# A one-core transformer layer: half 0 of its first projection without GpSimd, x's second half loaded later, and the later adaLN pieces summed or read out one step later

## The chip, the cores and the metric

The kernel runs on one core of a Trainium2 chip. The metric is the time of one execution in microseconds (us). A core has TensorE (PE in the profile), VectorE (DVE), ScalarE (ACT), GpSimd (POOL) and SyncE (SP), which here only issues loads and stores. All work on SBUF and, for matmul results, on PSUM; each engine takes its own instructions strictly in order and waits for others by semaphores.

## What is computed

One layer with 1024 tokens of width 1024, all in float32. A conditioning vector c gives six modulation vectors; x is normalised, scaled and shifted, goes through one input projection (for forgetting attention: fq, fk, fv, og and 8 forget columns; for retention: rq, rk, rv, rg; 512 columns each), two kinds of attention, an output projection and a squared-ReLU MLP.

```python
c_act = jax.nn.silu(c)
mod = jnp.einsum('bd,de->be', c_act, w_ada[l]) + b_ada[l]
shift_m, scale_m, gate_m, shift_f, scale_f, gate_f = jnp.split(mod, N_MOD, axis=-1)
h = _rms(x) * (1.0 + scale_m) + shift_m
proj = jnp.einsum('bsd,de->bse', h, w_in[l])
...  # forgetting attention on fq fk fv, retention on rq rk rv, gated by og and rg
x = x + gate_m * jnp.einsum('bse,ed->bsd', mixed, w_out[l])
h = _rms(x) * (1.0 + scale_f) + shift_f
u = jnp.square(jax.nn.relu(jnp.einsum('bsd,df->bsf', h, w_mlp_in[l])))
x = x + gate_f * jnp.einsum('bsf,fd->bsd', u, w_mlp_out[l])
```

## The kernel before

**Matmuls.** A float32 product is made as three products of halves: each operand is split into a rounded part (hi) and a remainder (lo), and PE adds hi x hi, hi x lo and lo x hi into one PSUM bank (L291 to L293). `split_w` makes the two halves of a tile of w_in: ACT casts the hi half (L134), DVE or POOL subtracts it for the lo half (L135).

**The first block.** Eight pieces `wam` of w_ada (k = 0 to 7, shift and scale columns of one block of 128, 1 MB each as two loads, L174) are summed on DVE with the elements of c as factors (`ada_sum`: L208 twice, L211 six times, then L573), and PE sums over the partitions with a column of ones (`ada_cols`, L217 to `mps`); DVE adds the bias (L219). x comes in four pairs of 128-token tiles (`load_x`, L183, two loads of 512 KB each). `norm_x` squares a tile on ACT (L248), and DVE and POOL make its factor (L249, L131), which DVE applies (L251). `make_hT(k, half)` transposes four tiles on PE (L263 to `tp`); ACT scales and shifts them into `h` (L265), DVE casts the hi half of `hT` (L267), and POOL subtracts for the lo half (L268). Then `proj_group("rg", ...)` runs over the eight k: four token tiles by three products, 12 matmuls in a step; half 0 is the first 512 tokens, half 1 the others. In half 0 the lo half of w_in's tiles is POOL's work, everywhere else DVE's. `first_stage(k)` is the hook that, one step ahead, loads piece k+4, sums piece k and makes its hT; at k = 2 and 3 it loads x's second half.

**The stages after it.** `forget_logits` (L396 to L409, `fp`), then rq, rk, rv, fq, fk, og, fv by the same routine, each two halves of eight steps, retention's chunks between them. The other 32 adaLN columns come meanwhile as 22 pieces `wa`: `plan(at, n, d_sum, d_col)` puts the load of a piece on step `at`, its sum on DVE (L232, L234) `d_sum` steps later, its column on PE (L239) and bias (L241) `d_col` steps later. Ten pieces are double (256 columns, 1 MB, two buffers), at every fourth step; twelve are single (512 KB, one buffer), at every fifth. Their loads are issued on ACT's queue (L229).

**What sets the order.** A list scheduler orders each engine's instructions from the program's data flow; `tc.keep_in_program_order` ties an instruction to its place in the code. From about 475 us on (the attention sweep) the order is written out by hand. SP's loads are issued in order too, and each waits for the eighth load before it. Buffers that loads and splits wait for: tiles of w_in (`raw`, two, each with two steps), split tiles (`f4`, five, which the retention gain and the rotary table `cs` share).

Of the kernel before, what the change touches and what calls it, by code (L numbers as in the profile page):

```python
# [13 lines left out]
AF = mybir.ActivationFunctionType  # L14
ALU = mybir.AluOpType
# [9 lines left out]
FH, FD = 8, 64  # L25
# [24 lines left out]
def tile_block(  # L50
# [20 lines left out]
    V, A, G, T, Q = nc.vector, nc.scalar, nc.gpsimd, nc.tensor, nc.sync  # L71
# [21 lines left out]
    def f32(ap):  # L93
        return ap.bitcast(F32)
# [10 lines left out]
    def cols(n):  # L105
        used[0] += n
        return sm[:, used[0] - n : used[0]]

    ones, mhalf, e_base, qkg, kgc, bfc = (cols(1) for _ in range(6))
    r_x, c_sb, c_act = cols(8), cols(8), cols(8)  # L110
    rc = cols(12)
# [7 lines left out]
    def mod(m, k):  # L119
        return mcol[:, 8 * m + k : 8 * m + k + 1]  # L120
# [12 lines left out]
    def split_w(raw_ap, h_ap, l_ap, eng=V):  # L133
        A.copy(h_ap, raw_ap)  # L134
        eng.tensor_tensor(l_ap, raw_ap, f32(h_ap), op=ALU.subtract)  # L135
# [23 lines left out]
    def rbank(name):  # L159
        turn.append(turn.pop(0))  # L160
        return turn[-1](name)
# [9 lines left out]
    def load_ada_m(k):  # L171
        ada_m[k] = s8([P, 8, 2, P], f"wam{k}")
        for m in range(2):
            Q.dma_start(ada_m[k][:, :, m, :], wada_v[:, :, m * D + k * P : m * D + (k + 1) * P])  # L174
# [5 lines left out]
    def load_x(g):  # L180
        xg[g] = s8([P, 2, D], f"x{g}")
        for i in range(2):
            Q.dma_start(xg[g][:, i, :], x_v[g][:, i, :])  # L183
# [21 lines left out]
    def ada_sum(w):  # L205

        for j in range(2):
            V.tensor_scalar(w[:, j], w[:, j], c_act[:, j : j + 1], None, op0=ALU.mult)  # L208
        for j in range(2, 8):
            a = w[:, j % 2]  # L210
            V.scalar_tensor_tensor(a, w[:, j], c_act[:, j : j + 1], a, op0=ALU.mult, op1=ALU.add)  # L211
# [9 lines left out]
    def ada_stages(m, k, n):  # L221


        w = (mr if n > 1 else ra)([P, 8, n * P], f"wa{m}_{k}")

        def load():

            at = m * D + k * P
            tc.keep_in_program_order(A.dma_start(w, wada_v[:, :, at : at + n * P]))  # L229

        def sums():
            tc.keep_in_program_order(V.tensor_scalar(w[:, 0], w[:, 0], c_act[:, 0:1], None, op0=ALU.mult))  # L232
            for j in range(1, 8):
                V.scalar_tensor_tensor(w[:, 0], w[:, j], c_act[:, j : j + 1], w[:, 0], op0=ALU.mult, op1=ALU.add)  # L234

        def cols_():
            ps = xbank(f"mps{m}_{k}")
            for i in range(n):
                T.matmul(ps[:, i : i + 1], w[:, 0, i * P : (i + 1) * P], ones, start=True, stop=True)  # L239
            at = slice(8 * m + k, 8 * m + k + n)  # L240
            V.tensor_tensor(mcol[:, at], ps[:, 0:n], bT[:, at], op=ALU.add)  # L241

        return load, sums, cols_
# [11 lines left out]
    def make_hT(k, half):  # L255

        if k not in hT:
            hT[k] = s8([P, 2, S], f"hT{k}", F32R)
        ht = hT[k]
        tp = rbank(f"tp{k}_{half}")  # L260
        for i in range(4):
            t = 4 * half + i
            T.transpose(tp[:, i * P : (i + 1) * P], xg[t // 2][:, t % 2, k * P : (k + 1) * P], ident)  # L263
        h32 = t2([P, CH], f"h32_{k}_{half}")
        A.activation(h32, tp, AF.Identity, bias=mod(0, k), scale=mod(1, k))  # L265
        hs = slice(half * CH, (half + 1) * CH)
        V.tensor_copy(ht[:, 0, hs], h32)  # L267
        G.tensor_tensor(ht[:, 1, hs], h32, f32(ht[:, 0, hs]), op=ALU.subtract)  # L268

    def load_win(k, col, name):  # L270
        wr = raw([P, 2, CH], f"wr_{name}_{k}")
        Q.dma_start(wr, win_v[:, k : k + 2, col : col + CH])
        return wr

    def proj_group(name, col, half, evac, hook=None, banks=None):

        toks = range(4 * half, 4 * half + 4)
        ps, wr = {}, None
        for k in range(NK):
            if hook:  # L280
                hook(k)
            if k % 2 == 0:
                wr = early.pop(0) if early else load_win(k, col, f"{name}{half}")
            ws = f4([P, 2, CH], f"ws_{name}{half}_{k}", F32R)
            split_w(wr[:, k % 2, :], ws[:, 0, :], ws[:, 1, :], G if name == "rg" and half == 0 else V)
            for n, t in enumerate(toks):
                if k == 0:
                    ps[t] = (banks[n] if banks else bank)(f"pp_{name}_{t}")
                hh = hT[k][:, 0, t * P : (t + 1) * P]
                hl = hT[k][:, 1, t * P : (t + 1) * P]  # L290
                T.matmul(ps[t], hh, ws[:, 0, :], start=(k == 0), stop=False)  # L291
                T.matmul(ps[t], hh, ws[:, 1, :], start=False, stop=False)
                T.matmul(ps[t], hl, ws[:, 0, :], start=False, stop=(k == NK - 1))  # L293
        for t in toks:
            evac(t, ps[t])
# [5 lines left out]
    def copy_out(t, dst, src):  # L301
        if t % 2 == 0:
            A.copy(dst, src)
        else:
            V.tensor_copy(dst, src)
# [4 lines left out]
    def nat_tile(name, t):  # L310
        if (name, t // 4) not in nat:
            nat[name, t // 4] = s8([P, 4, CH], f"{name}{t // 4}")
        return nat[name, t // 4][:, t % 4, :]
# [33 lines left out]
    tabs = {}  # L347

    def evac_rope(name):
        def go(t, ps):  # L350
            d = nat_tile(name, t)
            if name == "rk":

                V.tensor_tensor(
                    d.rearrange("p (h d) -> p h d", d=RD),
                    ps.rearrange("p (h d) -> p h d", d=RD),
                    rc[:, 0:4].unsqueeze(2).to_broadcast([P, RH, RD]),
                    op=ALU.mult,
                )
            else:  # L360
                copy_out(t, d, ps)
            dv = d.rearrange("p (a d) -> p a d", d=64)
            ac = r2([P, 2 * RH, 64], f"ac_{name}{t}")
            as_ = r2([P, 2 * RH, 64], f"as_{name}{t}")
            cs = tabs["cs"]
            G.tensor_tensor(ac, dv, cs[:, t, 0:64].unsqueeze(1).to_broadcast([P, 2 * RH, 64]), op=ALU.mult)
            G.tensor_tensor(as_, dv, cs[:, t, 64:128].unsqueeze(1).to_broadcast([P, 2 * RH, 64]), op=ALU.mult)
            V.tensor_tensor(dv[:, 0::2, :], ac[:, 0::2, :], as_[:, 1::2, :], op=ALU.subtract)
            V.tensor_tensor(dv[:, 1::2, :], as_[:, 0::2, :], ac[:, 1::2, :], op=ALU.add)

        return go

    def load_gain(g):
        t = f4([P, CH], f"gain_{g.tensor.name}")
        Q.dma_start(t, g.partition_broadcast(P))
        return t
# [139 lines left out]
    ret = retention()  # L516
# [6 lines left out]
    def plan(at, n, d_sum, d_col):  # L523
        m, k = cols_left[0]
        del cols_left[:n]
        stages = []

        def begin():
            stages.extend(ada_stages(m, k, n))
            stages[0]()  # L530

        todo[at].append(begin)
        todo[at + d_sum].append(lambda: stages[1]())
        todo[at + d_col].insert(0, lambda: stages[2]())

    for n in range(10):
        plan(4 * n, 2, 4, 6)
    for n in range(12):
        plan(41 + 5 * n, 1, 3, 5)
    assert not cols_left  # L540
    todo = [[]] + todo

# [20 lines left out]
        return go  # L563

    def first_stage(k):
        if k == 2:
            load_x(2)
        if k == 3:
            load_x(3)
        if k + 4 < NK:  # L570
            load_ada_m(k + 4)
        ada_sum(ada_m[k])
        V.tensor_tensor(ada_m[k][:, 0], ada_m[k][:, 0], ada_m[k][:, 1], op=ALU.add)  # L573
        ada_cols(ada_m[k], [0, 1], k, 1)
        make_hT(k, 0)

    for t in range(4):
        norm_x(t)
    tabs["ret"] = load_gain(ret_gain)
    proj_group("rg", OFF_R + 3 * RW, 0, evac_rg, ahead(first_stage))  # L580
    for t in range(4, NT):
        norm_x(t)
    proj_group("rg", OFF_R + 3 * RW, 1, evac_rg, ahead(lambda k: make_hT(k, 1)))
    Q.dma_start(rc, rconst)
    for r in range(2):
        Q.dma_start(qkg[r * FD : (r + 1) * FD, :], q_gain.unsqueeze(1))
        Q.dma_start(kgc[r * FD : (r + 1) * FD, :], k_gain.unsqueeze(1))
    Q.dma_start(bfc[:FH, :], b_forget.unsqueeze(1))
    V.scalar_tensor_tensor(qkg, qkg, 1.0 / math.sqrt(FD), kgc, op0=ALU.mult, op1=ALU.mult)
    tabs["cs"] = f4([P, NT, P], "cs")  # L590
    Q.dma_start(tabs["cs"], rope.rearrange("(t p) e -> p t e", p=P))
# [464 lines left out]
    for e in range(NE):  # L1056
# [25 lines left out]
        for fs in steps:  # L1082
            ws = [load_up(e * FPE + f, n == 2) for n, f in enumerate(fs)]
# [113 lines left out]
```

## Time and profile before

| | us |
|---|---|
| median of three runs (1399.49 to 1404.02) | 1403.5 |
| the profiled execution | 1402.06 |
| its span | 1400.3 |
| PE busy | 1330.4 |
| DVE busy | 867.7 |
| POOL busy | 599.5 |
| ACT busy | 459.1 |

The span is the time between the first and the last instruction that the profiler saw; the execution is 1.8 us longer. PE is busy for 95% of it. So of any stretch the first thing to read is how much of it PE stands still, and then which engine or load it waits for.

### The profile page before, as it was taken

Reading aid. Unit: us, or ns where it says so; the run is one execution under the profiler, and the core shown is the slowest. Engines: PE = TensorE matmul, PEld = TensorE weight load, DVE = VectorE, ACT = ScalarE, POOL = GpSimd, SP = SyncE. Lnnn points to the kernel's source line nnn. Section 1 sums busy time; section 2 is a strip of 40 time slices with the busy share of each in tenths; the row PEclk is TensorE's granted clock in tenths of the full one; section 3 lists DMA queues with packets and bytes.
Section 4 is the critical chain, followed back from the end, with each engine's and each line's share of the span. In section 5 each row is a group of like instructions: output and inputs, shape, how many; then the busy total and the mean of one; then the engine's idle time right before and its main releaser. Section 6 shows DMA issues by size and latency. Waiting matters only on the chain.

```text
span 1400.3 us, 16776 instructions
## 1 busy us (share of the span) xinstructions
PE 1330.4 (95%) x6325; PEld 1075.8 (77%) x6325; DVE 867.7 (62%) x1433; ACT 459.1 (33%) x741; POOL 599.5 (43%) x420
## 2 busy tenths in 40 slices
PE   5799999999998889999999999999999999999998
PEld 4678778878886666668877887887878788787886
DVE  6867997465564457763586927447283663827446
ACT  3342212243332357662343313223231222313222
POOL 3568452145631012232469552807337171552803
PEclk9899999999999999999999999999999999999999
DMA  9656576534357645752251211121121111211103
GB/s 271 202 118 157 153 180 136 136 91 134 115 135 177 162 117 126 244 215 76 91 181 31 75 30 31 60 61 60 31 61 47 44 61 46 75 31 30 61 8 113
DMA packets 120034, 146.09 MB, mean 104 GB/s; under 512 B 7464, under 2 KB 84344, under 8 KB 118928
## 3 DMA queue, kind: packets, MB, share of 16 engines
q1 hardware_dynamic: 97072, 128.23, 33.1%
q10 hardware_dynamic: 22880, 16.78, 3.9%
q8 instruction: 50, 0.82, 0.2%
q14 instruction: 32, 0.26, 0.1%
HBM read 122.85 MB, written 10.60 MB: 95 GB/s over the span
## 4 chain that ended last, share of the span: by engine, by line
PE 49%; DVE 4%; ACT 2%; POOL 1%; issue 1%; DMA 0%; ACTq 0%; POOLq 0%; DVEq 0%
PE X L1106 11%; PE up L1049 8%; PE up L1050 8%; PE up L1051 8%; PE Y L1106 6%; PE Z L1106 2%; PE po_woA L944 1%; PE po_woA L943 1%; PE po_woA L945 1%; ACT sa L1095 1%; DVE x L1120 1%; DVE sa L1096 1%; ACT sb L1095 1%; PE av L746 1%; POOL x L950 0%
## 5 line engine op out<-in xcount | busy, mean ns | idle before, releaser
L1049 PE MATMUL up<-h,wuh 128*128 128x512 f32 x496 | 193.1, 390 | 0.7 <-ACT h L994 0.7
L1050 PE MATMUL up<-h,wuh 128*128 128x512 f32 x496 | 193.0, 389 | 0.0
L1106 PE MATMUL X<-sb,sa 128*128 128x512 f32 x768 | 187.4, 394 | 5.4 <-ACT sb L1095 3.3
L1051 PE MATMUL up<-h,wul 128*128 128x512 f32 x496 | 192.1, 389 | 0.0
L1106 PEld LDWEIGHTS X<-sb,sa 128*128 128x128 f32 x768 | 144.2, 189 | 41.0 <-ACT sb L1095 5.8
L1096 POOL TENSOR_TENSOR sb<-wd,sb 128x1024 fp32r<-128x1024 f32 x48 | 125.1, 2607 | 65.0 <-ACT sb L1095 65.0
L1096 POOL TENSOR_TENSOR sb<-wt,sb 128x1024 fp32r<-128x1024 f32 x8 | 20.1, 2512 | 278.4 <-ACT sb L1095 278.4
L131 POOL TENSOR_TENSOR sm<-sm 128x8 f32<-128x8 f32 (+2 forms) x48 | 59.4, 1242 | 144.1 <-DVE sm L496 55.1
L1120 DVE TENSOR_TENSOR x<-X,x 128x512 f32<-128x512 f32 x128 | 84.6, 683 | 55.0 <-PE X L1106 55.0
L1096 DVE TENSOR_TENSOR sa<-u,sa 128x1024 fp32r<-128x1024 f32 x56 | 105.8, 1890 | 17.7 <-ACT sa L1095 17.7
L1049 PEld LDWEIGHTS up<-h,wuh 128*128 128x128 f32 x496 | 93.0, 188 | 20.2 <-ACT wuh L134 0.9
L1050 PEld LDWEIGHTS up<-h,wuh 128*128 128x128 f32 x496 | 93.1, 188 | 19.4 <-DVE h L995 0.2
L1051 PEld LDWEIGHTS up<-h,wul 128*128 128x128 f32 x496 | 93.1, 188 | 19.3
L1054 DVE SCALAR_TENSOR_TENSOR u<-up,rl 128x512 f32<-128x512 f32 x64 | 43.9, 687 | 98.7 <-ACT rl L1053 98.7
L135 DVE TENSOR_TENSOR wul<-wu,wuh 128x1024 fp32r<-128x1024 f32 x31 | 43.1, 1391 | 98.5 <-ACT wuh L134 91.0
L1095 ACT CAST sa<-u 128x1024 fp32r<-128x1024 f32 x56 | 58.6, 1051 | 134.6 <-PE X L1106 83.3
L1106 PE MATMUL Y<-sb,sa 128*128 128x512 f32 x384 | 91.4, 391 | 4.2 <-ACT sb L1095 4.2
L1106 PEld LDWEIGHTS Y<-sb,sa 128*128 128x128 f32 x384 | 71.6, 188 | 21.4 <-ACT sb L1095 6.8
L1095 ACT CAST sb<-wd 128x1024 fp32r<-128x1024 f32 x48 | 50.3, 1049 | 112.5 <-PE X L1106 74.8
L1071 POOL TENSOR_TENSOR wd<-wd,gf 128x1024 f32<-128x1024 f32 x32 | 83.0, 2617 | 0.8 <-DMA wd<-in_w_mlp_out_dram 0.8
L1053 ACT ACTIVATE rl<-up 128x512 f32<-128x512 f32 x64 | 38.0, 595 | 113.4 <-PE up L1051 113.3
L234 DVE SCALAR_TENSOR_TENSOR wa<-wa,sm 128x128 f32<-128x128 f32 (+1 forms) x154 | 69.4, 452 | 3.1
(285 smaller groups left out, 2953.0 us busy)
## 6 DMA issues: line engine op xcount, KB each, us to landing
wu<-in_w_mlp_in_dram SPq DMA_DIRECT2D x32, 512.0 KB, 4.1
wd<-in_w_mlp_out_dram SPq DMA_DIRECT2D x16, 1024.0 KB, 5.5
wa<-in_w_ada_dram ACTq DMA_DIRECT2D x10, 1024.0 KB, 6.0
wam<-in_w_ada_dram SPq DMA_DIRECT2D x16, 512.0 KB, 7.3
wa<-in_w_ada_dram ACTq DMA_DIRECT2D x12, 512.0 KB, 6.9
x<-in_x_dram SPq DMA_DIRECT2D x8, 512.0 KB, 7.3
wr_rq<-in_w_in_dram SPq DMA_DIRECT2D x8, 512.0 KB, 5.3
wr_rk<-in_w_in_dram SPq DMA_DIRECT2D x8, 512.0 KB, 4.0
```

What stands on the lines that cost most here:

```text
L131: G.tensor_tensor(ap, ap, mhalf.to_broadcast([P, n]), op=ALU.pow)
L135: eng.tensor_tensor(l_ap, raw_ap, f32(h_ap), op=ALU.subtract)
L234: V.scalar_tensor_tensor(w[:, 0], w[:, j], c_act[:, j : j + 1], w[:, 0], op0=ALU.mult, op1=ALU.add)
L1049: T.matmul(ps, wh[:, k, :], hh, start=(k == 0), stop=False)
L1050: T.matmul(ps, wh[:, k, :], hl, start=False, stop=False)
L1051: T.matmul(ps, wl[:, k, :], hh, start=False, stop=(k == NK - 1))
L1054: V.scalar_tensor_tensor(u, ps, 0.0, rl, op0=ALU.max, op1=ALU.mult)
L1071: gated = G.tensor_tensor(w, w, gf, op=ALU.mult)
L1095: A.copy(s[:, 0], v)
L1096: eng.tensor_tensor(s[:, 1], v, f32(s[:, 0]), op=ALU.subtract)
L1106: T.matmul(banks[i], sa[:, pa, a, ii], sb[:, pb_, a, :], start=(first and a == 0 and m == 0), stop=(a == 1 and m == 2), skip_group_check=n ...
L1120: V.tensor_tensor(xs, banks[i], xs, op=ALU.add)
```

## The change

It has four parts. First, in the first block: ACT makes the hi half of hT by a second activation from the same PSUM tile, in the place of DVE's cast, and DVE makes the lo half in the place of POOL; DVE also takes the lo halves of w_in's tiles in half 0. Second, x's second half is loaded by `first_stage(4)` and `(5)`, behind the w_ada pieces, and the retention gain by `first_stage(6)`. Third, six loads of small constants are tied to their place in the code. Fourth, the column of a double piece comes seven steps after its load (before: six), and the sum of a single piece four steps after it (before: three). Lines of the new kernel stand two or three higher from L262 on (L573 is L576 there).

```diff
--- before.py
+++ after.py
@@ -262,10 +262,10 @@
             t = 4 * half + i
             T.transpose(tp[:, i * P : (i + 1) * P], xg[t // 2][:, t % 2, k * P : (k + 1) * P], ident)
         h32 = t2([P, CH], f"h32_{k}_{half}")
-        A.activation(h32, tp, AF.Identity, bias=mod(0, k), scale=mod(1, k))
         hs = slice(half * CH, (half + 1) * CH)
-        V.tensor_copy(ht[:, 0, hs], h32)
-        G.tensor_tensor(ht[:, 1, hs], h32, f32(ht[:, 0, hs]), op=ALU.subtract)
+        for dst in (h32, ht[:, 0, hs]):
+            A.activation(dst, tp, AF.Identity, bias=mod(0, k), scale=mod(1, k))
+        V.tensor_tensor(ht[:, 1, hs], h32, f32(ht[:, 0, hs]), op=ALU.subtract)
 
     def load_win(k, col, name):
         wr = raw([P, 2, CH], f"wr_{name}_{k}")
@@ -282,7 +282,7 @@
             if k % 2 == 0:
                 wr = early.pop(0) if early else load_win(k, col, f"{name}{half}")
             ws = f4([P, 2, CH], f"ws_{name}{half}_{k}", F32R)
-            split_w(wr[:, k % 2, :], ws[:, 0, :], ws[:, 1, :], G if name == "rg" and half == 0 else V)
+            split_w(wr[:, k % 2, :], ws[:, 0, :], ws[:, 1, :])
             for n, t in enumerate(toks):
                 if k == 0:
                     ps[t] = (banks[n] if banks else bank)(f"pp_{name}_{t}")
@@ -369,6 +369,9 @@
             V.tensor_tensor(dv[:, 1::2, :], as_[:, 0::2, :], ac[:, 1::2, :], op=ALU.add)
 
         return go
+
+    def pinned(dst, src):
+        tc.keep_in_program_order(Q.dma_start(dst, src))
 
     def load_gain(g):
         t = f4([P, CH], f"gain_{g.tensor.name}")
@@ -534,9 +537,9 @@
         todo[at + d_col].insert(0, lambda: stages[2]())
 
     for n in range(10):
-        plan(4 * n, 2, 4, 6)
+        plan(4 * n, 2, 4, 7)
     for n in range(12):
-        plan(41 + 5 * n, 1, 3, 5)
+        plan(41 + 5 * n, 1, 4, 5)
     assert not cols_left
     todo = [[]] + todo
 
@@ -563,12 +566,12 @@
         return go
 
     def first_stage(k):
-        if k == 2:
-            load_x(2)
-        if k == 3:
-            load_x(3)
         if k + 4 < NK:
             load_ada_m(k + 4)
+        if k in (4, 5):
+            load_x(k - 2)
+        if k == 6:
+            tabs["ret"] = load_gain(ret_gain)
         ada_sum(ada_m[k])
         V.tensor_tensor(ada_m[k][:, 0], ada_m[k][:, 0], ada_m[k][:, 1], op=ALU.add)
         ada_cols(ada_m[k], [0, 1], k, 1)
@@ -576,16 +579,15 @@
 
     for t in range(4):
         norm_x(t)
-    tabs["ret"] = load_gain(ret_gain)
     proj_group("rg", OFF_R + 3 * RW, 0, evac_rg, ahead(first_stage))
     for t in range(4, NT):
         norm_x(t)
     proj_group("rg", OFF_R + 3 * RW, 1, evac_rg, ahead(lambda k: make_hT(k, 1)))
-    Q.dma_start(rc, rconst)
+    pinned(rc, rconst)
     for r in range(2):
-        Q.dma_start(qkg[r * FD : (r + 1) * FD, :], q_gain.unsqueeze(1))
-        Q.dma_start(kgc[r * FD : (r + 1) * FD, :], k_gain.unsqueeze(1))
-    Q.dma_start(bfc[:FH, :], b_forget.unsqueeze(1))
+        pinned(qkg[r * FD : (r + 1) * FD, :], q_gain.unsqueeze(1))
+        pinned(kgc[r * FD : (r + 1) * FD, :], k_gain.unsqueeze(1))
+    pinned(bfc[:FH, :], b_forget.unsqueeze(1))
     V.scalar_tensor_tensor(qkg, qkg, 1.0 / math.sqrt(FD), kgc, op0=ALU.mult, op1=ALU.mult)
     tabs["cs"] = f4([P, NT, P], "cs")
     Q.dma_start(tabs["cs"], rope.rearrange("(t p) e -> p t e", p=P))
```

Where instructions move, three places show it. SP's loads of the first block come first (`wam` are the pieces of w_ada, `wr_rg_2` the w_in tile of steps 2 and 3, `wr_rg_0` the last one named the first of half 1; L588 is the last of the six small constants, which stand in one row there). Before:

```order
L588 DMA sm<-in_b_forget_dram 8x1
L174 DMA wam_172<-in_w_ada_dram 128x8x128 x2
L272 DMA wr_rg_4_373<-in_w_in_dram 128x2x512
L183 DMA x_218<-in_x_dram 128x1024 x2
L174 DMA wam_221<-in_w_ada_dram 128x8x128 x2
L183 DMA x_263<-in_x_dram 128x1024 x2
L174 DMA wam_266<-in_w_ada_dram 128x8x128 x2
L272 DMA wr_rg_6_453<-in_w_in_dram 128x2x512
```

After:

```order
L174 DMA wam_143<-in_w_ada_dram 128x8x128 x2
L272 DMA wr_rg_2_285<-in_w_in_dram 128x2x512
L174 DMA wam_170<-in_w_ada_dram 128x8x128 x2
L272 DMA wr_rg_4_371<-in_w_in_dram 128x2x512
L174 DMA wam_216<-in_w_ada_dram 128x8x128 x2
L174 DMA wam_258<-in_w_ada_dram 128x8x128 x2
L272 DMA wr_rg_6_453<-in_w_in_dram 128x2x512
L378 DMA gain_in_ret_out_gain_dram<-in_ret_out_gain_dram 128x512
L272 DMA wr_rg_0_536<-in_w_in_dram 128x2x512
L183 DMA x_302<-in_x_dram 128x1024 x2
L183 DMA x_344<-in_x_dram 128x1024 x2
```

The constants are gone from between the pieces (they follow the last w_in tile of half 1). The gain, which stood ahead of piece 4 (`wam_145`), and both x pairs stand behind the pieces.

The second place is the step from rq to rk, on ACT, where casts of split tiles and the loads of double pieces stand in one row. Before:

```order
L134 CAST ws_rq_4_1079<-wr_rq_4_1077 128x512
L229 DMA wa_6_1102<-in_w_ada_dram 128x8x256
L134 CAST ws_rq_5_1104<-wr_rq_4_1077 128x512
L134 CAST ws_rq_6_1121<-wr_rq_6_1119 128x512
L134 CAST ws_rq_7_1140<-wr_rq_6_1119 128x512
L134 CAST ws_rk_0_1190<-wr_rk_0_1188 128x512
L134 CAST ws_rk_1_1219<-wr_rk_0_1188 128x512
```

After:

```order
L134 CAST ws_rq_4_1079<-wr_rq_4_1077 128x512
L134 CAST ws_rq_5_1104<-wr_rq_4_1077 128x512
L134 CAST ws_rq_6_1121<-wr_rq_6_1119 128x512
L134 CAST ws_rq_7_1136<-wr_rq_6_1119 128x512
L229 DMA wa_6_1102<-in_w_ada_dram 128x8x256
L134 CAST ws_rk_0_1190<-wr_rk_0_1188 128x512
L134 CAST ws_rk_1_1219<-wr_rk_0_1188 128x512
```

The load of `wa_6` moved behind the cast of rq's last step; on DVE its sum starts behind the split of rk's first step in both orders. On PE its column moved. Before:

```order
L292 MATMUL pp_rq_1012<-ws_rq_7_1140,hT_443 128x512
L293 MATMUL pp_rq_1012<-ws_rq_7_1140,hT_443 128x512
L451 MATMUL rqp_1731<-ident,rq_939 128x128 x4
L239 MATMUL mps_6_1251<-sm,wa_6_1102 128x1 x2
L291 MATMUL pp_rk_1193<-ws_rk_0_1190,hT_162 128x512
```

After:

```order
L291 MATMUL pp_rk_1205<-ws_rk_3_1251,hT_275 128x512
L292 MATMUL pp_rk_1205<-ws_rk_3_1251,hT_275 128x512
L293 MATMUL pp_rk_1205<-ws_rk_3_1251,hT_275 128x512
L239 MATMUL mps_6_1266<-sm,wa_6_1102 128x1 x2
L291 MATMUL pp_rk_1193<-ws_rk_4_1272,hT_319 128x512
```

It stood ahead of rk's first products, and stands ahead of those of step 4 now.

The third place is DVE from og to fv, where a single piece is summed among the splits of w_in. Before:

```order
L135 TENSOR_TENSOR ws_og_7_3366<-wr_og_6_3341,ws_og_7_3366 128x512
L135 TENSOR_TENSOR ws_fv_0_3399<-wr_fv_0_3397,ws_fv_0_3399 128x512
L241 TENSOR_TENSOR sm<-mps_5_3304,sm 128x1
L510 TENSOR_TENSOR mixr_2824<-rmp_2993,mixr_2824 128x512
L135 TENSOR_TENSOR ws_fv_1_3423<-wr_fv_0_3397,ws_fv_1_3423 128x512
L232 TENSOR_SCALAR wa_6_3307<-wa_6_3307,sm 128x128
L234 SCALAR_TENSOR_TENSOR wa_6_3307<-wa_6_3307,sm 128x128 x4
L135 TENSOR_TENSOR ws_fv_2_3440<-wr_fv_2_3438,ws_fv_2_3440 128x512
L234 SCALAR_TENSOR_TENSOR wa_6_3307<-wa_6_3307,sm 128x128 x3
L135 TENSOR_TENSOR ws_fv_3_3455<-wr_fv_2_3438,ws_fv_3_3455 128x512
```

After:

```order
L241 TENSOR_TENSOR sm<-mps_5_3304,sm 128x1
L135 TENSOR_TENSOR ws_og_7_3358<-wr_og_6_3341,ws_og_7_3358 128x512
L232 TENSOR_SCALAR wa_6_3307<-wa_6_3307,sm 128x128
L234 SCALAR_TENSOR_TENSOR wa_6_3307<-wa_6_3307,sm 128x128
L135 TENSOR_TENSOR ws_fv_0_3399<-wr_fv_0_3397,ws_fv_0_3399 128x512
L234 SCALAR_TENSOR_TENSOR wa_6_3307<-wa_6_3307,sm 128x128 x3
L467 TENSOR_TENSOR rkT_2875<-rip_2894,tri 128x512
L234 SCALAR_TENSOR_TENSOR wa_6_3307<-wa_6_3307,sm 128x128 x3
L135 TENSOR_TENSOR ws_fv_1_3423<-wr_fv_0_3397,ws_fv_1_3423 128x512
L135 TENSOR_TENSOR ws_fv_2_3440<-wr_fv_2_3438,ws_fv_2_3440 128x512
```

The sum of `wa_6` stood behind the second split of fv, and stands ahead of the first one now; on ACT its load moved from behind the cast of fv's first tile to behind that of og's last.

## Rows read from the trace of the kernel before

**Rows 1.** Page, section 1: busy time, share of the span, instructions:

```profile
PE 1330.4 (95%) x6325; PEld 1075.8 (77%) x6325; DVE 867.7 (62%) x1433; ACT 459.1 (33%) x741; POOL 599.5 (43%) x420
```

**Rows 2.** Busy time by stretch: start:end, length, engines, PEclk, DMA, GB/s:

```profile
0.00:25.00 25.00, 10.46 (x33) 7.63 (x34) 14.16 (x40) 8.00 (x13) 7.63 (x15) 1.00 0.97 277
20.00:30.00 10.00, 7.57 (x28) 6.43 (x27) 10.00 (x30) 1.02 (x2) 1.65 (x2) 0.91 1.18 303
20.00:65.00 45.00, 35.17 (x134) 27.59 (x132) 41.63 (x92) 13.18 (x22) 20.97 (x17) 0.81 0.82 232
74.00:95.00 21.00, 21.00 (x94) 17.36 (x93) 14.93 (x18) 8.18 (x14) 12.87 (x10) 1.00 0.44 84
110.00:250.00 140.00, 133.02 (x615) 109.67 (x615) 120.20 (x198) 34.58 (x59) 70.85 (x56) 0.99 0.65 159
```

**Rows 3.** Waits of PE, 0 to 110 us: total us, times, longest us:

```profile
PE mps L217 <- DVE wam L573: 11.8, 3, 7.7
```

**Rows 4.** Time line of PE, half 0: start us, us, line, idle before:

```profile
64.69 0.61 PE L217 MATMUL mps<-sm,wam 128*128 128x1 f32 x4 [1.61 <-DVE wam L573]
...
70.84 1.18 PE L293 MATMUL pp_rg<-ws_rg,hT 128*128 128x512 f32 x4
```

**Rows 5.** Waits of PE, 110 to 475 us:

```profile
PE mps L239 <- issue: 4.7, 3, 2.0
PE pp_fv L292 <- DVE ws_fv L135: 3.8, 1, 3.8
PE pp_fk L291 <- DVE fq L333: 3.4, 1, 3.4
```

**Rows 6.** Waits of DVE, 230 to 480 us:

```profile
DVE wa L232 <- DMA wa<-in_w_ada_dram: 33.9, 10, 7.7
```

**Rows 7.** Instructions by line, 7 to 72 us: busy us, mean ns:

```profile
L211 DVE SCALAR_TENSOR_TENSOR wam<-wam,sm 128x256 f32<-128x256 f32 x48 | 27.3, 623 | 0.0
...
L268 POOL TENSOR_TENSOR hT<-h,hT 128x512 fp32r<-128x512 f32 x10 | 14.3, 1434 | 17.4 <-DVE hT L267 17.4
...
L265 ACT ACTIVATE h<-tp,sm 128x512 f32<-128x512 f32 x12 | 9.1, 776 | 28.7 <-DVE sm L219 24.8 <-PE tp L263 4.0
...
L135 POOL TENSOR_TENSOR ws_rg<-wr_rg,ws_rg 128x512 fp32r<-128x512 f32 x6 | 8.6, 1453 | 6.5 <-ACT ws_rg L134 6.5
...
L267 DVE CAST hT<-h 128x512 fp32r<-128x512 f32 x12 | 7.4, 629 | 3.0 <-ACT h L265 3.0
...
L135 DVE TENSOR_TENSOR ws_rg<-wr_rg,ws_rg 128x512 fp32r<-128x512 f32 x3 | 4.2, 1403 | 0.0
```

**Rows 8.** Time line of DVE, first block:

```profile
34.47 1.51 DVE L573 TENSOR_TENSOR wam<-wam 128x256 f32<-128x256 f32 x1
...
37.05 1.66 DVE L211 SCALAR_TENSOR_TENSOR wam<-wam,sm 128x256 f32<-128x256 f32 x4
...
39.17 0.41 DVE L573 TENSOR_TENSOR wam<-wam 128x256 f32<-128x256 f32 x1
...
44.03 0.41 DVE L267 CAST hT<-h 128x512 fp32r<-128x512 f32 x1
...
49.66 0.35 DVE L208 TENSOR_SCALAR wam<-wam,sm 128x256 f32<-128x256 f32 x1
...
64.56 0.68 DVE L135 TENSOR_TENSOR ws_rg<-wr_rg,ws_rg 128x512 fp32r<-128x512 f32 x1
```

**Rows 9.** Time line of POOL, the same time:

```profile
34.23 2.89 POOL L135 TENSOR_TENSOR ws_rg<-wr_rg,ws_rg 128x512 fp32r<-128x512 f32 x2
```

**Rows 10.** Time line of SP, which issues loads (us held at the issue):

```profile
26.86 0.47 SPq L584 DMA_DIRECT2D sm<-in_rconst_dram  x1
...
39.38 3.62 SPq L183 DMA_DIRECT2D x<-in_x_dram  x2
43.04 1.64 SPq L174 DMA_DIRECT2D wam<-in_w_ada_dram  x2
```

**Rows 11.** Page, section 6: loads by issue: KB each, median us to landing:

```profile
wa<-in_w_ada_dram ACTq DMA_DIRECT2D x10, 1024.0 KB, 6.0
```

## The prediction

> **What bounds the kernel now.** I read the busy shares first. TensorE (PE below) works 1330.4 us, 95% of the span [rows 1], so a change gains only where PE stands still. The table by stretch [rows 2] says where: from 20 to 65 us PE has 35.17 of 45 at a granted clock of 0.81 (part of it at 1.2, the rest at 2.4 GHz), from 74 to 95 us 21.00 of 21, from 110 to 250 us 133.02 of 140. In the first stretch VectorE (DVE) has 41.63 of 45: it sets the end. PE's own waits agree, 11.8 us of them before the column product of a w_ada piece (`mps`) until the last sum of that piece (L573) is done [rows 3]. The chain to follow is: w_ada pieces land, DVE sums them, PE makes the column, h is scaled, the projection step runs. Its last link shows on PE's own time line [rows 4]: the column of piece 7 starts at 64.69 us after a wait for L573, and the last products of half 0 end about 72.0 us. From 110 to 475 us the list of PE's waits holds 4.7 us before `mps` of a later adaLN piece, 3.8 before fv and 3.4 before fk [rows 5]; behind the last two stands DVE, which waits 33.9 us in ten places for a w_ada piece (`wa`) to land, with the next splits queued behind it [rows 6]. From about 475 us on the code order is the same, and I cost that part at nothing.
>
> **GpSimd leaves half 0.** Taken away from GpSimd (POOL): 16 subtractions of make_hT at 1.43 us and 8 splits of w_in at 1.45 [rows 7]. POOL's own time is worth nothing; what counts is that DVE runs slower beside it. Three undisturbed and one disturbed row show it [rows 8]: L211 takes 1.66/4 = 0.415 us, the cast L267 0.41, a split L135 0.68, L573 0.41, but 1.51 at 34.47 us, under two POOL splits of 2.89 us from 34.23 [rows 9]. Against these, the rows of 7 to 72 us [rows 7] hold too much: L211 27.3 - 48 x 0.415 = 7.4 us; L267 7.4 - 12 x 0.41 = 2.5; L135 on DVE 4.2 - 3 x 0.68 = 2.2. Together 12.1, of which I put 2.5 behind 65 us (casts and splits of half 1), and 1.1 for the L573 above: 10.7 come back. Added to DVE are 8 splits, 8 x 0.68 = 5.4, and in half 0 eight subtractions in the place of eight casts, 8 x (0.68 - 0.41) = 2.2 (a subtraction with two sources priced as the split, its nearest row). Sum on DVE up to piece 7: 41.6 - 10.7 + 5.4 + 2.2 = 38.5 us.
>
> ACT gets 16 activations from PSUM at 0.78 us [rows 7], 8 of them in half 0: 6.2 us, beside an engine that is busy 13.18 of 45 us there [rows 2]. It costs on the path only 0.8 us a step where the next cast of w_in stands behind it, and saves the cast's 0.41 between ACT and PE; I take zero, with -1 to +1.
>
> What the 34.47 row tells of the manner: two POOL splits of 2.89 us put 1.1 us on L573 and can put at most as much again on what follows, so DVE is slowed for part of a POOL operation, not for the whole of it, and I stay with the measured 10.7 us. The Trainium skill ("SBUF — State Buffer", section "SBUF: two separate sides") says otherwise: a GpSimd operation and a DVE operation with two SBUF sources take a shared port as a lock, for a whole instruction. By that rule the sum would have up to 21.8 us in the place of 10.7 (rival b has the working).
>
> **Loads in another order.** In the order before, x's third pair goes out ahead of piece 6 and the fourth, at 39.38 us, ahead of piece 7, which is issued at 43.04; the six constants stand from 26.86 us among the w_ada loads [rows 10]. Afterwards pieces 4 to 7 come first, then wr_rg_6, the gain, the first w_in tile of half 1, then both x pairs. By 25 us 25 x 0.277 = 6.9 MB have moved [rows 2]. Up to piece 7 the new order needs 12.1 MB (8.4 of w_ada, 2.1 of x, 1.6 of w_in); at 0.303 MB/us (20 to 30 us, [rows 2]) it lands at 25 + 5.2/0.303 = 42 us, against a first sum at 49.66 before [rows 8]. To the last x it is 15.5 MB: 25 + 8.6/0.303 = 53 us; at the mean of 20 to 65 us, 0.232 [rows 2], 62 us. The x loads also stand behind wr_rg_0' in SP's order, which wants the split of step 5 on DVE done; by the order on DVE I put that at 40 us, so bandwidth, not the queue, sets 53.
>
> So DVE no longer waits for piece 7 (its idle time from 20 to 65 us is 45 - 41.6 = 3.4; I keep 1.5 for x). Its sums end at 20 + 38.5 + 1.5 = 60 instead of 64.7: 4.7 us earlier. PE cannot follow much faster: the x squares stand ahead of h5 to h7 on ACT, x is there at 53, so h5 is ready at 54, and three steps of 12 products at 21.00/94 = 0.223 us [rows 2], 2.7 us each, with transposes and columns end about 64.5 to 66. Half 1 runs without a gap before (21.00 of the 21 us from 74 on [rows 2]), and I expect the same afterwards. **First block: 5 us gained**, at most 8 (72 to 64), at least 1 (x at 62 us instead of 53 delays h7 by up to 9 and leaves little). The pinned constants come behind wr_rg_6' and are wanted after half 1: nothing, hidden by the 21 us of half 1; the table cs and the forget weights issued behind them lose some 3 us of their slack, which costs nothing unless `fp` starts over 3 us late.
>
> **Pieces summed a step later.** A double piece gives its column one step later (at +7): the 4.7 us of `mps` waits [rows 5] go. But DVE works 120.20 of 140 us there [rows 2], so PE meets it soon after; I give it half, 2.5. A single piece is summed at +4 where it was at +3; it is 0.5 MB and its load is on ACT's queue. In the orders above, the piece before fv is loaded one cast earlier, and the piece that held up the fq copies is summed behind them. A step is 2.7 us. Of the 3.8 before fv and 3.4 before fk I count 5 of the 7.2 as gone. New waits: the sum stands nearer its column, and the splits queued behind L232 are those of fv0, two steps sooner than before; 0 to 3 us, of which I take 0.5. **Second part: 2.5 + 5 - 0.5 = 7 us**, at most 12 (all of these 11.9 us), at least 2.
>
> **The rivals.** (a) Only the first block gains: DVE waits for `wa` at other splits and PE loses the 7 us elsewhere. For it: the waits of 33.9 us have their cause in the landing, which nobody shortens. 1402 - 5 = 1397 us. (b) All of it: if a POOL operation holds DVE up for its whole length, the some 15 of 1.45 us that lie before 65 us [rows 7] were worth 21.8 us to DVE, not 10.7; its sums then end 11 us sooner, and the first block comes to the 8 us that x allows. With 12 of the second part that is 20 us, 1382. The page of the Trainium skill named above would have it so. (c) x comes late: SP's order puts it behind three loads that wait for buffers; if the split of step 5 is done only at 48 us, x's last half lands near 62, h7 waits for it, and half 0 ends as before. The second part's lower half remains: about 1400. (d) Slower: in the new order seven of the double pieces are loaded one cast ahead of the split that their sum follows (before: two and four in turn), so DVE, which takes them in order, can stand 6.0 (landing of a 1 MB piece, [rows 11]) - 2.7 = 3.3 us in front of each, 23 us in all. DVE has 140 - 120.2 = 19.8 us to spare in that stretch, and the splits run up to four steps ahead of PE, which speaks against it; but the table cs holds one of the five buffers. If 13 of the 23 us reach PE, the time is 1402 - 5 + 13 = 1410; from 9 us on the whole is measurably slower.
>
> **How the numbers follow.** The profiled run took 1402.06 us (span 1400.3), 1.4 under the median 1403.5 of the three runs; the sum is made against 1402. Forecast: 1402 - 5 - 7 = 1390, and I put 1391 because a few tenths of every stall stay. Differences under 0.3%, about 4 us, can hardly be told from none. Chances: forecast (1384 to 1398) 0.55; (a) 1397, 0.15; (b) 1382, 0.10; (c) 1400, 0.11; (d) 1410, 0.09. The range 1382 to 1401 takes in the forecast, (a), most of (c) and the upper half of (b), about 0.83. Faster by over 0.3%: 0.55 + 0.14 + 0.10 - 0.02 = 0.77; slower 0.09; the same 0.14.
>
> **What would show it.** Right in the first block: DVE shows no L211 over 0.45 us, POOL nothing between 20 and 70 us but L131, the wait of `mps` for L573 falls from 11.8 to under 7, the last products of half 0 end at 64 to 67 us and half 1 ends near 90 us, not 95. Wrong there: ACT's squares wait for x past 55 us, or PE's transposes of half 1 do. Right in the second part: the rows of fv and fk [rows 5] are gone or under 1 us each, and 110 to 250 us hold at least 3 us more PE work per time. Wrong: the wait of DVE for `wa` grows beyond 34 us in the stretch 110 to 250 us and PE waits for `ws_rk` or `ws_rv` splits by several us. If from 475 us on the two traces differ in length by more than 1 us, something not named here is at work.

## The result

The changed kernel takes 1387.86 us in the median of four runs (1385.1 to 1389.66), against 1402.47 of the kernel before: a ratio of 0.9901, with a 95% interval of 0.9882 to 0.9919. That is a gain of 13.9 us (11.4 to 16.5 by the interval); 1391 us was forecast, with 1382 to 1401 as the range. The profiled execution took 1387.09 us, with a span of 1385.4.

The table by stretch answers to [rows 2] (columns as there, PE, PEld, DVE, ACT, POOL, then clock, DMA share, GB/s):

```profile
20.00:30.00 10.00, 6.58 (x28) 5.25 (x29) 8.91 (x26) 1.45 (x2) 0.00 (x0) 1.00 1.19 301
20.00:65.00 45.00, 35.04 (x157) 28.37 (x158) 38.09 (x101) 22.57 (x37) 2.92 (x4) 0.89 0.88 246
74.00:95.00 21.00, 20.27 (x95) 14.85 (x95) 10.12 (x18) 9.79 (x16) 4.97 (x4) 1.00 0.74 153
110.00:250.00 140.00, 130.77 (x607) 106.04 (x606) 111.98 (x192) 33.32 (x57) 64.89 (x56) 1.00 0.59 149
```

DVE has 38.09 us of work in 20 to 65 us where it had 41.63 [rows 2]; POOL has 2.92 where it had 20.97. From 110 to 250 us, where the prediction wanted at least 3 us more PE work, there is less: 130.77 against 133.02. The same groups of instructions as in [rows 7], 7 to 67 us (busy us, mean ns):

```profile
L211 DVE SCALAR_TENSOR_TENSOR wam<-wam,sm 128x256 f32<-128x256 f32 x48 | 20.8, 480 | 0.0
...
L268 DVE TENSOR_TENSOR hT<-h,hT 128x512 fp32r<-128x512 f32 x10 | 6.9, 689 | 2.9 <-ACT hT L267 2.9
...
L135 DVE TENSOR_TENSOR ws_rg<-wr_rg,ws_rg 128x512 fp32r<-128x512 f32 x9 | 6.1, 688 | 0.7 <-ACT ws_rg L134 0.5
```

L211 fell from 27.3 us busy to 20.8, 0.433 for each of the 48 (the mean of 480 ns counts the stretch in which two neighbours overlap twice). The end of half 0 and its neighbours, as in [rows 4], then the waits of PE, as in [rows 3] and [rows 5]:

```profile
54.76 0.50 PE L291 MATMUL pp_rg<-ws_rg,hT 128*128 128x512 f32 x1 [2.32 <-ACT hT L267]
...
56.93 0.50 PE L217 MATMUL mps<-sm,wam 128*128 128x1 f32 x4
...
63.64 1.18 PE L293 MATMUL pp_rg<-ws_rg,hT 128*128 128x512 f32 x4
```

```profile
PE mps L217 <- DVE wam L576: 11.1, 2, 7.9
PE pp_rg L291 <- ACT hT L267: 4.2, 4, 2.3
```

```profile
PE pp_rk L292 <- DVE ws_rk L135: 3.7, 4, 1.5
...
PE pp_rk L291 <- DVE rk L354: 1.0, 1, 1.0
PE pp_rv L291 <- DVE rv L305: 0.9, 1, 0.9
...
PE pp_fv L292 <- DVE ws_fv L135: 0.2, 1, 0.2
```

Piece 7's column is made at 56.93 us (before 64.69), half 0 ends at 64.8 (before 72.0), and PE's waits before the later `mps` (4.7 us) and before fk (3.4) have no row any more; fv's 3.8 are 0.2. In their place stand several waits in rk and rv; the largest row is 3.7 us, in four waits of 1.5 us at most.

Where each stage starts, by the first matmul into the stage's PSUM bank in PE's time line (us), and by how much earlier:

| stage | before | after | earlier |
|---|---|---|---|
| fp (end of half 1) | 95.37 | 89.95 | 5.4 |
| rk | 151.07 | 143.72 | 7.4 |
| rv | 202.85 | 198.17 | 4.7 |
| fq | 257.45 | 252.67 | 4.8 |
| fk | 315.61 | 309.01 | 6.6 |
| og | 375.39 | 364.60 | 10.8 |
| S (attention sweep) | 474.24 | 460.26 | 14.0 |
| av | 498.18 | 482.80 | 15.4 |
| MLP (`up`) | 721.47 | 706.50 | 15.0 |

So the first block gave 5.4 us, rq and what follows up to fq lost 0.6, and fq to S gave 9.2 (216.8 us long before, 207.6 after). Half 0 itself ends 7.2 us sooner; of these 0.9 go in half 1, which takes 24.4 us and not 23.5, and 0.9 at its end, where fp now waits 0.7 us for DVE.

### The profile page after: what moved, and what is told of

The parts are those of the page before. It is cut to its first block, busy times and chain, and to the rows that moved or that the text cites. A ratio compares the mean times of both kernels' runs of the same rounds, so it can differ in the third digit from the quotient of the medians.

```text
span 1385.4 us, 16767 instructions
## 1 busy us (share of the span) xinstructions
PE 1318.4 (95%) x6325; PEld 1065.8 (77%) x6325; DVE 859.0 (62%) x1441; ACT 470.1 (34%) x757; POOL 565.9 (41%) x396
## 4 chain that ended last, share of the span: by engine, by line
PE 50%; DVE 4%; ACT 2%; POOL 1%; issue 1%; DMA 0%; ACTq 0%; POOLq 0%; DVEq 0%
PE X L1108 11%; PE up L1051 8%; PE up L1052 8%; PE up L1053 8%; PE Y L1108 6%; PE Z L1108 2%; PE po_woA L946 1%; PE po_woA L945 1%; PE po_woA L947 1%; ACT sa L1097 1%; DVE x L1122 1%; DVE sa L1098 1%; ACT sb L1097 1%; PE av L748 1%; POOL x L952 0%
```

## The experiments

Theory: the four parts add up, the first three as 5.4 us of the first block, the single pieces as 9 us, the double pieces as nothing. Rivals: the double pieces give or cost something of their own; one part alone makes the first block's gain; the parts need one another. Each kernel is told by its difference from the one before or from the changed one.

**The first three parts without the plan.**

```diff
 (the changed kernel)
-        plan(4 * n, 2, 4, 7)
+        plan(4 * n, 2, 4, 6)
...
-        plan(41 + 5 * n, 1, 4, 5)
+        plan(41 + 5 * n, 1, 3, 5)
```

> The kernel before with the first three parts (GpSimd out of half 0, x and gain loaded later, constants tied), the later adaLN pieces as before. Theory, that the parts add up: the first block alone gives 5.4 us, so about 1397; fp starts near 90 us and every later stage is 5.4 us early, the attention sweep (S) at about 469. Rival, that the later stages gave what they gave only because the first block released something (buffers, the order of loads): S at 461 to 465 and 1388 to 1392 us.

Measured: 1396.62 us, ratio 0.9977 (0.9962 to 0.9991), a gain of 3.2 us. S at 471.2, 3.0 us early, far from the rival's 461 to 465: the later stages' gain is not the first block's. But fp came at 94.11 in this execution, not at the theory's 90, with the same order of instructions up to there. ACT and PE in the two executions, the changed kernel's ACT first:

```profile
49.48 1.06 ACT L248 ACTIVATE xsq<-x 128x1024 f32<-128x1024 f32 x1 [2.63 <-DMA x<-in_x_dram]
```

```profile
52.08 1.06 ACT L248 ACTIVATE xsq<-x 128x1024 f32<-128x1024 f32 x1 [2.77 <-DMA x<-in_x_dram]
```

```profile
57.36 0.50 PE L291 MATMUL pp_rg<-ws_rg,hT 128*128 128x512 f32 x1 [3.15 <-ACT hT L267]
57.70 0.39 PE L292 MATMUL pp_rg<-ws_rg,hT 128*128 128x512 f32 x1
...
58.70 0.63 PE L291 MATMUL pp_rg<-ws_rg,hT 128*128 128x512 f32 x1
```

x's third pair landed 2.6 us later; h5 stands behind its squares on ACT, PE waited 3.15 us, and then its products follow one another at 0.43 us, not 0.23: the lower of its two clocks. So 2.6 us of landing became 4.2 at fp.

**The double pieces' column alone, and its undoing.**

```diff
 (the kernel before; no_double is the changed kernel with +6 again)
-        plan(4 * n, 2, 4, 6)
+        plan(4 * n, 2, 4, 7)
```

> The kernel before with only the double pieces' column at +7. Theory, that VectorE is the limit there: the three waits of PE before mps (4.7 us) go and come back as waits for splits of rk and rv, so 1402 within 1.5 us, rv starting within 1 us of 202.9. Rival, the prediction's own term: 2.5 us and up to 4.7, so 1398 to 1400, rv at 198 to 200.

> The changed kernel with the double pieces' column back at +6. Theory: 1388 within 1.5 us, the mps waits of rk and rv are back and the waits for ws_rk gone. Rival: the double pieces' step is worth its 2.5 us, 1390.5; or it costs, since rk lost 2.7 us of the lead in the changed kernel: 1386.

Measured: alone 1406.61 us, ratio 1.0043 (1.0028 to 1.0058), slower; undone in the changed kernel 1385.81, ratio 0.9898 (0.9882 to 0.9914), which cannot be told from the changed one's 0.9901 (the theory wanted 1388 within 1.5 us; the time lies at the second rival's 1386). PE's waits from 100 to 475 us, alone and then undone:

```profile
PE pp_rk L292 <- DVE ws_rk L135: 3.5, 3, 1.5
PE pp_rv L291 <- DVE rk L354: 1.1, 1, 1.1
PE pp_rk L291 <- DVE rq L305: 0.9, 2, 0.7
```

```profile
PE mps L239 <- issue: 4.1, 3, 2.0
PE pp_rk L292 <- DVE ws_rk L135: 2.5, 1, 2.5
```

The `mps` waits go and come back as waits for splits, copies and rope products of DVE, as the theory had it, but for one wait of 2.5 us for `ws_rk` that stays when the step is undone. Alone, it is worse than the theory's 1402. In the profiled execution S is 4.2 us late, 2.3 of which stand at fp already, where the order is still the old one; I count some 2 us on the part itself there, and what the other runs have beyond that is open.

**The single pieces alone.**

```diff
 (the kernel before)
-        plan(41 + 5 * n, 1, 3, 5)
+        plan(41 + 5 * n, 1, 4, 5)
```

> The kernel before with only the single pieces summed at +4. Theory: the gain behind the first block is theirs, 9 us: 1393, with rv at 202.9 as before, and from fq to S about 208 us in the place of 216.8. Rival, that the waits for landing pieces move only: 4.5 us (the prediction's term) or less, 1398 to 1402.

Measured: 1390.73 us, ratio 0.9932 (0.9914 to 0.995), a gain of 9.5 us; rv at 203.3 and fq to S 207.6 us. The theory's figure holds, the prediction's 4.5 is too small. DVE's waits, as in [rows 6]:

```profile
DVE wa L232 <- DMA wa<-in_w_ada_dram: 21.5, 7, 5.0
```

12.4 of the 33.9 us of waiting [rows 6] went. What PE's two stalls cost beyond their length stands in the trace of the kernel before (one stretch by the table, and PE's time line in it):

```profile
314.00:322.00 8.00, 6.39 (x19) 5.12 (x20) 4.15 (x12) 0.95 (x3) 6.30 (x7) 0.57 0.23 66
```

```profile
315.61 0.80 PE L291 MATMUL pp_fk<-ws_fk,hT 128*128 128x512 f32 x1 [3.39 <-DVE fq L333]
316.21 0.63 PE L292 MATMUL pp_fk<-ws_fk,hT 128*128 128x512 f32 x1
316.63 0.63 PE L293 MATMUL pp_fk<-ws_fk,hT 128*128 128x512 f32 x1
```

After the 3.39 us without work the granted clock is 0.57 over the stretch, and 12 products take 5.3 us instead of 2.8: at 1.2 GHz, not 2.4. Behind the 3.84 us before fv the slow products come a little later:

```profile
433.52 0.40 PE L293 MATMUL pp_fv<-ws_fv,hT 128*128 128x512 f32 x1
...
434.55 0.63 PE L291 MATMUL pp_fv<-ws_fv,hT 128*128 128x512 f32 x1
434.98 0.63 PE L292 MATMUL pp_fv<-ws_fv,hT 128*128 128x512 f32 x1
```

Eight products run so from 434.2 us on, 1.5 us more than at full speed. So the two stalls of 7.2 us cost 11.2, of which 9.2 (fq to S in the changed kernel) to 9.5 (this run) came back.

**Each of the first three parts alone.**

```diff
 gpsimd_only: the first part of the change alone, on the kernel before
 x_order_only: its second part alone (first_stage, load_gain)
 pin_only: its third part alone (pinned)
```

> The kernel before with the first part alone: no GpSimd in half 0, x and the constants where they were. Theory, that the landing of piece 7 at 49.7 us then sets the end of half 0: what comes back is only the slowing after that, some 3 to 4 us, 1397 to 1398, L211 at 0.43 us in the mean and fp at 91 to 92. Rival, that VectorE's time as a whole sets it (the prediction's sum 10.7 - 7.6): 3 us too, but spread, with no idle time of VectorE before piece 7; told apart by the wait of L208 for its load, 5 us or more by the theory, under 2 by the rival.

> The kernel before with x's second half and the gain loaded later alone. Theory, that the slowed VectorE sets it: piece 7 lands near 43 us but is summed only at 60 to 62, 1399 to 1401, fp at 93 to 95. Rival, that the load was the limit: as much as the whole first block, fp at 90, 1396.

> The kernel before with only the six constants tied to their place. Theory (the prediction costs them at nothing): the same time within 2 us, fp within 1 us of 95.4. Rival, that the 3.8 us they hold the load queue come back: pieces 5 to 7 land 3 us sooner and fp at 92 to 93, 1398.

Measured: 1404.26 us, ratio 1.0006 (0.9993 to 1.0018); 1411.34, 1.0059 (1.0037 to 1.0081), slower; 1402.01, 0.9992 (0.998 to 1.0004). The first two expectations fall; the third holds in the time, while its fp, at 96.5, is 1.1 us late and not within 1. Alone, no part gives anything, and the load order costs 8 us. The first part by itself does what it should on DVE (L211 at 0.44 us), but half 0 ends at 71.0 us, 1 us sooner than before, and then fp waits. The landing of piece 7, which the theory put in its way, is not the reason: L208 starts on piece 7 at 55.16 us without a wait. Four splits of w_in now stand among the sums of that piece on DVE, which end at 62.2 us (before 64.6). PE, and DVE at the forget weights (`wfr` is their tile as loaded, `wf` the split one), for gpsimd_only; then DVE for the changed kernel:

```profile
98.70 0.43 PE L406 MATMUL fp<-hT,wf 128*40 128x512 f32 x1 [2.67 <-DVE wf L399]
...
100.19 0.63 PE L406 MATMUL fp<-hT,wf 128*40 128x512 f32 x1
```

```profile
91.51 0.33 DVE L394 MEMSET wfr<- 128x320 f32 x1
...
97.58 0.33 DVE L398 CAST wf<-wfr 128x320 fp32r<-128x320 f32 x1 [2.88 <-DMA wfr<-in_w_in_dram]
```

```profile
79.80 0.33 DVE L397 MEMSET wfr<- 128x320 f32 x1
...
87.00 0.33 DVE L401 CAST wf<-wfr 128x320 fp32r<-128x320 f32 x1 [2.87 <-DMA wfr<-in_w_in_dram]
```

The tile is cleared on DVE before it is loaded. With either of the first two parts alone the scheduler puts the clearing (L394) behind the split of rq's first step; in gpsimd_only it then runs at 91.5 us, the weights land at 97.6, fp waits 2.67 us and is slowed by the lower clock (0.43 us a product where 0.23 are normal). In the changed kernel it stands ahead of that split, 79.8 us, and fp does not wait. x_order_only has the same place and one more wait, ACT for POOL's lo halves of half 1:

```profile
ACT h L265 <- POOL hT L268: 4.5, 2, 3.8
ACT ws_rg L134 <- POOL hT L268: 3.2, 1, 3.2
```

```profile
102.80 0.65 PE L406 MATMUL fp<-hT,wf 128*40 128x512 f32 x1 [3.17 <-DVE wf L399]
```

**The pins undone, and the forget weights early.**

```diff
 no_pin: the changed kernel without its third part
 gpsimd_wf: gpsimd_only with
-        wfr = t2([P, NK, 40], "wfr")
+        wfr = r2([P, NK, 40], "wfr")
```

> The changed kernel without the third part: the six constants are not tied, all else as changed. VectorE then clears the forget-weight tile behind the split of rq's first step, as in the kernels with one part alone, and ahead of it in the changed one. Theory, that this place decides: the forget weights are loaded near 92 us, fp waits some 3 us for them and runs its first products at the lower clock for 2 to 3 us more, 1392 to 1394. Rival, the prediction's own line that the pins are worth nothing: 1388 within 1.5 us and fp at 90.

> The first part alone (as gpsimd_only), and the tile of the forget weights taken from another pool, so that it is cleared and loaded early. Theory, that the late forget weights ate what the first part gives: fp without a wait at 95.5 to 96, rq's first product near 103 where gpsimd_only had 107.7, 1399 to 1400. Rival, that half 0 itself gained nothing (its last products at 72 us as before): then it is the time before, 1402, and not faster than that.

Measured: no_pin 1392.89 us, ratio 0.9935 (0.9918 to 0.9952). The theory's time holds: 5 us are lost, and the clearing stands behind the split of rq's first step again. DVE clears at 86.96 us, then:

```profile
93.89 0.65 PE L406 MATMUL fp<-hT,wf 128*40 128x512 f32 x1 [2.40 <-DVE wf L399]
94.33 0.63 PE L407 MATMUL fp<-hT,wf 128*40 128x512 f32 x1
```

fp waits 2.40 us, where it waits 0.7 in the changed kernel, and its first seven products run at 1.2 GHz (1.4 us more): the late clearing is worth some 3 us in this execution. The rest, about 2 us, stands before: the constants are among the pieces on the load queue again, x's loads are issued from 42.83 us on and not from 40.75, and x's first square of the third pair is at 51.46 us, not 49.48. That this 2 us is the constants' is not shown: kernels with pins have that square anywhere from 49.1 to 52.1 us (table below), and ACT's order differs here. So the pins work through the clearing, and perhaps through the queue; neither is seen with pins alone.

gpsimd_wf took 1403.19 us, ratio 1.0005 (0.9989 to 1.002): not the 1399 to 1400 of the theory. Its profiled execution, at 1398.59 us the fastest of ten, shows what was meant (fp at 95.09 without a wait for the weights, rq at 102.5 where gpsimd_only had 107.7); the other nine have no trace. Even there rq starts only 0.3 us ahead of the kernel before (102.8). This experiment is inconclusive: the late weights are a cost in the executions that were profiled, but not shown to be the whole of what the first part alone lacks.

**Two attempts at more.**

```diff
 squares_later: no_double, and in first_stage
-        if k in (4, 5):
-            load_x(k - 2)
         if k == 6:
+            load_x(2)
+            load_x(3)
             tabs["ret"] = load_gain(ret_gain)
 (and load_x tied to its place for g > 1)
 double_36: the changed kernel with
-        plan(4 * n, 2, 4, 7)
+        plan(4 * n, 2, 3, 6)
```

> The changed kernel with the double pieces at +6 again and x's second half tied to its place in first_stage(6); ScalarE then makes h5 and h6 ahead of the squares of x, the loads stand in the same row as before. Theory, that x's landing reaches half 0 only through the squares ahead of h5 to h7: h5 comes 2 to 3 us sooner, half 0 ends at 62 to 63 us, fp at 87 to 88.5, 1383 to 1384.5. Rival, that half 1 needs the squares at that time anyway: half 1 starts no sooner, fp at 89.5, 1386.

> The changed kernel with the double pieces summed at +3 and read out at +6 (before: +4, +6; changed: +4, +7). Theory, that the waits before mps come from sums that start too late for their column: they go without moving the column, 1383 to 1384.5. Rival, that VectorE is full there and only trades these waits for waits of splits: 1386 to 1388, as with the column moved.

> The changed kernel itself once more, for the comparison on one chip with double_36 and for the spread of its first block: 1388 within 1.5 us; fp between 89.5 and 94 us, by how early x's second half lands (first square of it between 49.5 and 52 us). If fp stays at 90 while x lands late, x is not what sets it.

Measured: squares_later 1386.63 us (0.9877, 0.9855 to 0.9898); double_36 1389.19 (0.9911, 0.9893 to 0.993); the changed kernel again 1387.86 (0.9896, 0.9878 to 0.9914). None can be told from the changed kernel. In squares_later half 0's last columns come sooner (it ends at 62.2 us, as its theory had it), and half 1 waits for x instead, as its rival said, with fp at 91.84, later than either had it:

```profile
55.36 0.50 PE L219 MATMUL mps<-sm,wam 128*128 128x1 f32 x4
...
63.57 0.55 PE L265 MATMUL tp<-ident,x 128*128 128x128 f32 x3 [1.05 <-DVE x L253]
65.50 0.50 PE L293 MATMUL pp_rg<-ws_rg,hT 128*128 128x512 f32 x1 [1.38 <-ACT hT L269]
...
91.84 0.42 PE L411 MATMUL fp<-hT,wf 128*40 128x512 f32 x1 [1.55 <-DVE gr L386]
```

In double_36 the waits of `mps` halve and splits are late instead, 3.8 and 3.0 us, as its rival said; the time is a little over the rival's 1386 to 1388:

```profile
PE pp_rk L292 <- DVE ws_rk L135: 3.8, 2, 3.6
PE pp_rq L292 <- DVE ws_rq L135: 3.0, 1, 3.0
PE mps L239 <- issue: 2.1, 1, 2.1
```

The repeat had x's first square at 50.73 us and fp at 92.80. Over the five executions whose first block has one and the same order:

| kernel | first square of x's third pair | fp |
|---|---|---|
| no_double | 49.06 | 89.53 |
| double_36 | 49.06 | 89.53 |
| changed | 49.48 | 89.95 |
| changed, again | 50.73 | 92.80 |
| first_block | 52.08 | 94.11 |

The later x lands, the later fp, by 4.6 us over 3.0: in the new order x's landing sets the first block.

Put together, the theory that the four parts add up holds between the two groups and not inside the first. The first three parts together (3.2 us) and the single pieces (9.5) make 12.7 us, against 13.9 in the changed kernel and 14.3 in no_double, within the intervals of these runs; the double pieces add nothing. The first three parts give their gain only together.

## Why the prediction was right, point by point

**The sum** was 5 + 7 = 12 us, 11 forecast; 13.9 were measured. That it came out so near is in part luck: the second half holds two errors of opposite sign, a gain from the double pieces that is not there and too small a gain from the single ones.

**DVE in half 0.** 38.5 us were worked out up to piece 7; the table above has 38.09 in 20 to 65 us. With the 7.6 us that were added by the prediction's estimate, 41.6 - 38.1 + 7.6 = 11.1 us came back, against 10.7 from the rows. The sums of piece 7 were done sooner than worked out, though, at 53.9 us and not at 60, since part of the 38.5 us (splits of half 1, tiles of x, the last subtractions) comes behind them in the order on DVE. What holds half 0 until 64.8 is the other limit that the prediction set, x's squares ahead of h5 to h7.

How POOL slows DVE stands in single rows of the kernel before, DVE first and then POOL:

```profile
50.60 1.52 DVE L211 SCALAR_TENSOR_TENSOR wam<-wam,sm 128x256 f32<-128x256 f32 x1
...
59.70 2.93 DVE L211 SCALAR_TENSOR_TENSOR wam<-wam,sm 128x256 f32<-128x256 f32 x2
```

```profile
50.50 1.34 POOL L268 TENSOR_TENSOR hT<-h,hT 128x512 fp32r<-128x512 f32 x1 [2.01 <-DVE hT L267]
...
59.40 2.94 POOL L135 TENSOR_TENSOR ws_rg<-wr_rg,ws_rg 128x512 fp32r<-128x512 f32 x2 [2.98 <-ACT ws_rg L134]
```

A single L211 takes 0.47 us undisturbed. Here it ends 0.28 us after POOL's subtraction (52.12 against 51.84), 1.05 us late, and the two L211 beside two subtractions lose 2.06 us. Twelve of the 13 subtractions between 19.9 and 65 us stretch one DVE instruction each in this way, 11.9 us in all; beside the other one DVE is idle. The Trainium skill ("SBUF — State Buffer", section "SBUF: two separate sides") says that a POOL operation and a DVE operation that has two SBUF sources or uses two ports take a shared port as a lock, for a whole instruction, and the other one waits. These rows agree with it. So rival (b) was too high in the price, about 1.0 us for each subtraction and not its full 1.45, and x, no longer DVE, sets the end of half 0.

**Loads.** x's loads were issued from 40.75 us on, as worked out (40); the first pair had landed by 49.5, the last tile no later than its square at 54.6 (53 forecast). Half 0 ended at 64.8 (64.5 to 66 forecast); half 1 ran almost without a gap, 20.27 of 21 us. The 5.4 us in the profiled pair of executions are the 5 forecast. What the step missed is that x has no slack left: rival (c), in part, is the spread of this order itself, 4.6 us at fp between the five executions of the table. By its ten runs, first_block gains 3.2 us, in the lower half of the 1 to 8 that were given.

**The pins** "nothing". Right alone (0.9992), wrong in this kernel: 5 us. The step looked at who waits for the constants, and not at whose place in the queues they take: x's, and through the scheduler the clearing of the forget weights' tile. What it said of the loads behind the constants held: in the changed kernel the forget weights are split at 88.1 us, 1.9 ahead of fp (before 6.1), and fp does not wait for them. Without the pins they come later, not sooner, and fp waits 2.4 us: the effect has the other sign from the one that was weighed.

**The double pieces**, 2.5 us of the 4.7. Measured: none in the changed kernel, a loss alone. The reason against was in the row that the step quoted, DVE at 120.2 of 140 us: every wait that goes before `mps` is paid again where PE next needs DVE. The half that I gave was a guess. Rival (d) had the sign of the double pieces but not their mechanism: DVE's wait for a landing double piece is 1.1 us in all from 100 to 255 us, not 23.

**The single pieces**, 5 - 0.5. Measured 9.2 to 9.5. Both stalls went whole, not 5 of 7.2; new waits are 0.2 (fv) and 0.6 (og); and the slower products after each stall were left out, 2.5 and 1.5 us, though [rows 2] already showed the granted clock below 1 where PE waits.

**The sign to look for** was badly chosen in one place: the wait of `mps` for L573 was to fall from 11.8 to under 7. It is 11.1, because 7.9 us of it are the first piece, at 11.6 us, which nothing here touches; of the 11.8 only 1.61 belonged to piece 7 [rows 4]. The time line, not the total, carried the argument. For the second part the signs were mixed: fk and fv came out as the right ones, while PE's work from 110 to 250 us (130.77, where at least 136 was wanted) and 3.7 us of waits for `ws_rk` spoke against the double pieces, as they should have.

**Behind 475 us** the two traces differ by 1.4 us between S and av (23.9 us long before, 22.5 after), over the 1 us that I allowed. Kernels whose order there is one and the same have 22.2 (the repeat) to 24.0 us (no_pin) in it, so this is spread; it stays unexplained.

## What to carry to other kernels

Price a stall of PE by its own length and by the products behind it: here 7.2 us of stalls cost over 11, and moving one operation by one step gave 9. Where a list scheduler sets the order, parts of a change do not add up: three parts worth +0.8, +8.3 and -1.1 us alone gave -3.2 together, because each moves other instructions too (here the clearing of a small tile, and x's squares ahead of h5). Alone, the first and the last of them cannot be told from nothing. So read the new order at every engine that waits, and undo parts before keeping all. Moving work to wait less for one engine pays only if that engine has time to spare where the work lands.

## What was not expected of the hardware

After 3.39 us without work PE ran 12 products at 0.43 us each (1.2 GHz) before it returned to 0.23; after 3.84 us, four products ran at full speed and only then eight slow ones. After the waits of 0.6 to 1.5 us in rk and rv of the changed kernel the granted clock stayed at 1.00 from 110 to 250 us. A POOL subtraction of 1.3 to 1.6 us costs DVE about 1.0 us, in one DVE instruction, which ends shortly after it (0.28 us for most, 0.55 for a subtraction on 512 columns); DVE's products from PSUM (L381, 0.67 to 0.69 us) ran inside POOL subtractions unslowed. One and the same program, with the same order, had x's first square of the third pair, which waits for its load, at 49.5 and at 50.7 us in two executions, and the second took 3 us longer.
